# One large matmul for the prompt and one small one for the samples, in eight tiles of a feed-forward layer

## The chip, the cores and the metric

The kernel runs on one core of a Trainium2 chip, in one launch. The metric is the device time of that launch in microseconds (us). Before the change it is 1905.85 us, the median of three runs.

## The reference, cut to what matters

The model is a decoder step of two layers for a prompt of 512 tokens and 8 samples of one token each, with shared weights. Each layer has a mixer and, after it, a SwiGLU feed-forward; RMSNorm stands before and after every block. The change touches the feed-forward of layer 0 alone.

```python
D_MODEL = 1024; SEQ = 512; DEC_BATCH = 8; DEPTH = 2
D_FF = -(-8 * D_MODEL // (3 * 256)) * 256          # 2816

def swiglu(h, w_gate, w_up, w_down):
    return (jax.nn.silu(h @ w_gate) * (h @ w_up)) @ w_down

# in the trunk, for every layer l
x = x + rmsnorm(m, norm_mix_post[l])
f = swiglu(rmsnorm(x, norm_ffn_pre[l]), w_ffn_gate[l], w_ffn_up[l], w_ffn_down[l])
x = x + rmsnorm(f, norm_ffn_post[l])
```

## The kernel before, in words

**Layout.** Activations lie feature-major: 128 features on the partitions, tokens along the free axis. The tokens are 520 columns, 512 of the prompt and 8 of the samples, worked on in two halves: columns 0 to 255 (256 wide) and columns 256 to 519 (264 wide, so the samples ride with the second half). `HALF` and `HW` (lines 24 and 25) hold these.

**Precision.** Every linear layer is done in three products to keep nearly full precision: weights and inputs are each split into hi + lo, both of type float32r (fp32r; the profile's matmul rows write f32), and hi'xh + hi'xl + lo'xh is summed. The inputs of the feed-forward lie in the buffers Hh (hi) and Hl (lo).

**A linear layer, `lin` (line 299).** One output tile is 128 output features for all tokens. Over the 8 row tiles of the 1024 inputs, over the three products, and over the two halves, one matmul each: 8 x 3 x 2 = 48 a tile, into two PSUM accumulators, one for each half. The weights are the stationary operand (128x128) and the tokens the moving one; each matmul instruction comes with its own weight load, and both halves of a product use the same weights, one right after the other. The accumulators come from `acc` (line 261): a ring of four PSUM buffers of 512 float32 a partition, a tile takes two of them. All matmuls are recorded at line 268, that of the helper `mm`.

**Weights, `WStream` (line 129).** SP loads weights in blocks of 1 MB, 256 output columns (two tiles) at a time, into a ring of two buffers (raw, line 138). ACT or DVE rounds 4 row tiles of them to hi (whi, lines 289 and 290), POOL or DVE makes lo (wlo, line 165); both rings have four buffers. To every few loads a copy of the samples' key and value caches, DRAM to DRAM, is tied on SP's queue (`copy_after`, line 1122).

**The feed-forward, `ffn` (line 1059).** It has 22 gate tiles and 22 up tiles, in 11 steps p of two tiles t each: gate tiles 2p and 2p + 1, then up tiles 2p and 2p + 1. The four tiles of p = 0 are made ahead by `group` (line 308), the first halves of all before the second halves. Gate tile t = 2 goes to a spare PSUM buffer, ma (`spare`, line 1076, with `ma_f0`); all later ones go to acc. After a gate tile, for each half: DVE multiplies it by the tokens' norm (line 1095), ACT takes silu of it (line 1097). After an up tile, for each half: DVE multiplies it by the gate's (line 1104), ACT rounds that to hi (line 1106), DVE makes lo (line 1107). In the profile these stand under the helpers' lines, 274 (`tt`) and 284 (`act`). The output projection `out_proj` (line 469) follows, with w_ffn_down.

**What sets the order.** The program is written in one order; a planner of the tile framework (`schedule_with_timeline_sim=True`, line 1882) sets the order on each engine by dependencies and modelled times. `high_priority` pulls the weight splits and the reads of PSUM ahead, `issue_after` holds an instruction behind another. TensorE's matmuls of this stage stand in the written order.

Of the kernel before, what the change touches and what calls it, by code (L numbers as in the profile page):

```python
# [11 lines left out]
F32R = mybir.dt.float32r  # L12
# [109 lines left out]
def KN(n, v, *others):  # L122
    """The engine, share or order chosen at a place: v unless the table has another of the choices."""
    return KNOBS.get(n, v)
# [4 lines left out]
class WStream:  # L129
    """Weights, in the order of use: loaded in groups, split into hi + lo in units of at most 4 row tiles."""  # L130
# [38 lines left out]
    def tile(s, ap, c0, kts, spread=None, ncol=None, out=None):  # L169
        """Yield (row tile, hi, lo) for the 128 columns from c0 and the row tiles kts; input weights come two tiles a load.  # L170
        out = (buffer, offset) of 1024 floats for each four row tiles, to hold them apart from the ring."""
        if ncol is None:
            g = c0 - c0 % 256
            if s.key != (ap.tensor.name, ap.offset, g):
                s.key, s.raw = (ap.tensor.name, ap.offset, g), s.load(ap, 0, 8, g, 256)
            raw, off = s.raw, c0 - g
        else:
            raw, off = s.load(ap, 0, 8, c0, ncol), 0
        for k0 in range(0, len(kts), 4):
            hi, lo = s.split(raw, kts[k0], 4, off, spread, out and out[k0 // 4])  # L180
            for j in range(4):
                yield kts[k0] + j, hi[:, j], lo[:, j]

    def rows(s, ap, c0, loads):
        """As tile() for a tall matrix; loads are (first row tile, count, unit offsets in their order)."""
        for k0, n, offs in loads:
            raw = s.load(ap, k0, n, c0, 128)
            for o in offs:
                m = min(4, n - o)
                hi, lo = s.split(raw, o, m, 0)  # L190
                for j in range(m):
                    yield k0 + o + j, hi[:, j], lo[:, j]


class Ker:
# [14 lines left out]
    def gen(s, *names):  # L210
        """From here on these buffers hold something else: float32r operands and float32 data never share a tile."""
        for n in names:
            s.big[n] = s.sb.tile([128, BIG[n]], F32, tag=n, name=n, bufs=1)

    def lay(s, name, off=0, n=KD, dt=F32R):
        """Operand (tile, half) -> columns, for n tiles of all tokens."""
        t = s.B(name, off, n, NT, dt=dt)
        return lambda k, h: t[:, k, HALF[h]]

    def layh(s, name, n=KD):  # L220
        """As lay(), the first half of the tokens of every tile before the second."""
        return lambda k, h: s.B(name, 256 * n * h + k * HW[h], HW[h], dt=F32R)
# [63 lines left out]
    def cp(s, e, out, in_):  # L286
        """Copy on ACT, DVE or GpSimd."""
        if e == "A":
            return s.nc.scalar.copy(out, in_).ins  # L289
        return (s.nc.vector if e == "V" else s.nc.gpsimd).tensor_copy(out, in_).ins  # L290
# [7 lines left out]
    # ---- linear layers: weights stationary, 520 token columns moving in two halves  # L298
    def lin(s, w, xh, xl, nkt, halves=(0, 1), ps=None):
        """ps[half] = sum over row tiles of w (yielding (row tile, hi, lo)) of hi'xh + hi'xl + lo'xh."""  # L300
        ps = ps or {h: s.acc()[:, 0:HW[h]] for h in halves}
        for n, (kt, hi, lo) in enumerate(w):
            for lhs, x, st, sp in ((hi, xh, n == 0, False), (hi, xl, False, False), (lo, xh, False, n == nkt - 1)):
                for h in halves:
                    s.mm(ps[h], lhs, x(kt, h), st, sp)
        return ps

    def group(s, w, xh, xl, nkt):
        """Up to four tiles, the first half of the tokens of all before the second half, which may come later."""
        w = [list(v) for v in w]  # L310
        ps = [{} for _ in w]
        for t in range(len(w)):
            if t % 2 == 0:
                a = s.acc()
            ps[t][0] = a[:, 256 * (t % 2):256 * (t % 2) + 256]
        for t in range(len(w)):
            ps[t][1] = (s.acc() if t < 2 else s.mx())[:, 0:HW[1]]
        for h in (0, 1):
            for t, v in enumerate(w):
                s.lin(v, xh, xl, nkt, (h,), ps[t])  # L320
        return ps

    def lnexp(s, ins):
        """After ins, one table load for Ln and Exp."""
# [3 lines left out]
    def rstd(s, out, ps, n, e=EPS, keep=None, after=None):  # L328
        """out = rsqrt(ps / n + e), refined by a Newton step; keep = EPS * (ps / n + e)."""
# [17 lines left out]
    # ---- setup  # L347
# [66 lines left out]
    def add_sq(s, h, x, first, tmp, eng=None):  # L414
        """accT += x^2."""
# [7 lines left out]
    def prenorm(s, n, l, hi, lo, h, upd=None):  # L423
        """hi + lo = x * gain, exactly split."""
# [9 lines left out]
    def token_norm(s, h, keep=None):  # L434
        """s.R2 = per-token rsqrt(mean x^2 + eps), on every partition."""
# [7 lines left out]
    def boundary(s, deferred):  # L443
        """x += mp * rsqrt(mean m^2 + eps), then the next layer's prenorm (n, l, hi, lo): the second half, and the norms."""
# [5 lines left out]
    def residual(s, deferred, h):  # L450
        """One half's update of x, as a function of the feature tile."""
# [17 lines left out]
    def out_proj(s, rows, xh, xl, nkt, mp, n, l, pre, tail=2, final=False):  # L469
        """mp = m * gain, accT + sqs = sum m^2 for the eight tiles of an output projection; the last ones by token halves."""  # L470
# [46 lines left out]
    # ---- causal convolution of one 128-feature tile, then silu  # L517
# [26 lines left out]
    def conv_sample(s, nt, new, old, w, bias, out, tmp):  # L544
        """new [128, nt, 8], old [128, nt, 8, 3], w(j) [128, nt]; out [128, nt, 8] = silu(conv)."""
# [12 lines left out]
    def gate_z(s, ps, zt):  # L558
        """zt = silu(z)."""
# [8 lines left out]
    def softplus(s, out, x, n):  # L568
        """out = max(x, 0) + log1p(exp(-|x|)); log1p(e) = 2 atanh(e / (2 + e)) as a series. Shapes [128, n]."""
# [16 lines left out]
    # ---- layer 0: input projection and mixers in the order of issue  # L586
# [78 lines left out]
    # ---- layer 0: sample convolution state  # L665
# [21 lines left out]
    # ---- layer 0: dt, decays in token layout  # L687
# [53 lines left out]
    # ---- layer 0: SSD over four chunks of 128 tokens, for one group of heads  # L741
# [78 lines left out]
    # ---- layer 0: one SSM step per sample  # L820
# [39 lines left out]
    # ---- layer 0: gate, grouped norm  # L860
# [6 lines left out]
    def l0_norm(s, g, zt, yh, yl):  # L867
        """y * silu(z) (in zt), normalised, to the exactly split yh + yl."""
# [11 lines left out]
    # ---- layer 0: attention of the prompt  # L880
# [25 lines left out]
    def l0_tokens(s, hp):  # L906
        """Keys and values token-major: the caches of the prompt and of the samples, V for the products."""
# [82 lines left out]
    # ---- layer 0: attention of the samples over their cached rows  # L990
# [67 lines left out]
    # ---- SwiGLU  # L1058
    def ffn(s, l):
# [4 lines left out]
        x = s.lay("Hh"), s.lay("Hl")  # L1064

# [21 lines left out]
        for p in range(11):  # L1087
            sg = {}
            for t in (2 * p, 2 * p + 1):
                ps = first[t] if p == 0 else s.lin(s.W.tile(g, 128 * t, kts), *x, 8, ps=spare(t < 2 + KN("ma_f%d" % l, 0, 1, 2)))  # L1090
                for h in (0, 1):
                    sl = (s.B("cs", NT * (t % 2), NT) if l == 0 else sgs if t % 2 else s.accT)[:, HALF[h]]
                    gt = s.tmp(HW[h])
                    with s.tc.high_priority():
                        s.tt(gt, ps[h], s.R2[:, HALF[h]], ALU.mult)
# [3 lines left out]
            for t in (2 * p, 2 * p + 1):  # L1099
                ps = first[2 + t] if 2 + t < len(first) else s.lin(s.W.tile(u, 128 * t, kts), *x, 8)  # L1100
                for h in (0, 1):
                    gt = s.tmp(HW[h])
                    with s.tc.high_priority():
                        s.tt(gt, sg[t, h], ps[h], ALU.mult)
# [9 lines left out]
    def cache_shift(s):  # L1114
        """The samples' rolling caches: all rows but the oldest move up by one."""
# [11 lines left out]
    def final_early(s):  # L1127
        """x and the norm's eps of the second half token-major."""
# [27 lines left out]
    def final_first(s):  # L1156
        """The first half's outputs; m of the second half token-major, as far as it is known."""
# [26 lines left out]
    def final_last(s):  # L1184
        """The second half's outputs, token-major: x + m * rsqrt(mean m^2 + eps)."""
# [19 lines left out]
    # ---- layer 1: gated delta net, input projection and mixer in the order of issue  # L1205
# [119 lines left out]
    def vo(s, g, h, j):  # L1325
        """Half h of the tokens of v head 8 g + j: V token-major, then the outputs feature-major."""
# [5 lines left out]
    # ---- layer 1: beta, decays in token layout  # L1332
# [41 lines left out]
    # ---- layer 1: keys (w = 0) and queries token-major: sums of squares, keys for the state products  # L1374
# [23 lines left out]
    def log_norm(s, g, w):  # L1398
        """-log(sum of squares + eps) / 2 in place, seen per v head."""
# [6 lines left out]
    def bcast_rows(s, t, tag):  # L1406
        """[tokens, 32] to DRAM as 32 rows of 128 tokens."""
# [14 lines left out]
    # ---- layer 1: the 32 (chunk, v head) systems of one half of the heads, I + strictly lower  # L1422
# [37 lines left out]
    # ---- layer 1: transposed unit-triangular inverses in place of the systems: diagonal blocks of 32 by elimination  # L1460
# [27 lines left out]
    # ---- layer 1: the inverses of 64 and 128 rows from those of 32  # L1488
# [57 lines left out]
    # ---- layer 1: delta rule over four chunks of 128 tokens, for one half of the heads  # L1546
# [119 lines left out]
    # ---- layer 1: silu(z) times the normalised outputs, split into hi + lo  # L1666
# [16 lines left out]
    # ---- layer 1: sample convolution state  # L1683
# [25 lines left out]
    # ---- layer 1: one delta-rule step per sample: what the states are not needed for  # L1709
# [42 lines left out]
    # ---- layer 1: one delta-rule step per sample: outputs, then (l1_sample_state) states  # L1752
# [133 lines left out]
```

## Time and profile before

| what | value |
|---|---|
| median of 3 runs | 1905.85 us (1904.42 to 1915.31) |
| profiled execution, span from the first to the last instruction | 1901.6 us |
| the same execution's time from end to end | not given by the page |
| mean granted TensorE clock | 0.965 |
| DMA, mean rate | 141 GB/s |
| HBM, read and written | 241.01 MB and 62.04 MB |

How to read the profile: PE is TensorE's matmul, PEld its weight load, DVE VectorE, ACT ScalarE, POOL GpSimd, SP SyncE. A row of instructions gives line, engine, operation, the tiles written and read (out<-in), their shapes (`128*128 128x256`: loaded weights of 128 rows and 128 columns, 256 columns moving), and their count (x). In the timeline the first number is the start and the second the length of the merged piece, both in us; instructions of one name that follow one another are merged into one row with the shape of the first, so that a pair of 256 and 264 columns shows as 256 x2. In the groups by form the numbers behind the bar are busy us, mean ns of one, and idle us before them. A matmul's recorded length holds its way through the array, and matmuls overlap: how fast they follow one another is read from starts and counts, not from that length. A recorded end is modelled.

### The profile page before, as it was taken

The page shows a single profiled execution, that of the slowest core. Times are in us where ns is not written, and L with a number is a line of the kernel's source. Part 1 is how long each engine was busy: PE and PEld are TensorE (multiplying, and loading weights), DVE is VectorE, ACT ScalarE, POOL GpSimd, SP SyncE. Part 2 cuts the span into 40 slices and gives each one's busy share as a digit, 9 for nine tenths or more (in the row PEclk, how much of TensorE's full clock was granted, in tenths as well). Part 3 has the DMA queues.
Part 4 walks back from the last instruction along what each step waited for, and adds up shares of the span by engine and source line. Part 5 has one row for each costly group of instructions (what it writes and reads, how often), then busy time and mean ns, then how long its engine had stood idle before and what let it go on. Part 6 is the DMA issues. An engine that isn't in the chain of part 4 may idle for free.

```text
span 1901.6 us, 36269 instructions
## 1 busy us (share of the span) xinstructions
PE 1746.8 (92%) x14263; PEld 1659.2 (87%) x14263; DVE 1190.0 (63%) x2334; ACT 748.7 (39%) x1828; POOL 876.2 (46%) x768
## 2 busy tenths in 40 slices
PE   8899999898999999988968898989889999999996
PEld 7888777698999999977857787978889899999996
DVE  6898878638323221178899977888954954443125
ACT  5432335555222223355756555544334511111222
POOL 2565756234444433435474554646668411112452
PEclk9999999998999999999988899999989899999998
DMA  7345765453333334453442123257998333432333
GB/s 259 125 130 183 237 202 142 145 182 113 111 111 112 112 106 136 124 177 114 137 139 72 59 65 92 63 156 212 272 290 237 132 135 134 134 133 84 92 92 106
DMA packets 293323, 268.88 MB, mean 141 GB/s; under 512 B 11841, under 2 KB 276742, under 8 KB 291986
## 3 DMA queue, kind: packets, MB, share of 16 engines
q1 hardware_dynamic: 292502, 265.90, 45.5%
q8 instruction: 112, 1.84, 0.4%
q10 hardware_dynamic: 652, 0.68, 0.1%
q14 instruction: 57, 0.47, 0.1%
HBM read 241.01 MB, written 62.04 MB: 159 GB/s over the span
## 4 chain that ended last, share of the span: by engine, by line
PE 56%; DVE 26%; DMA 8%; issue 4%; ACT 4%; POOL 2%; SPq 1%; DVEq 0%; POOLq 0%; ACTq 0%
PE acc L268 48%; DVE p L274 4%; DVE cs L281 4%; PE ma L268 4%; PE mb L268 3%; DVE b L274 2%; DVE sq L281 2%; DMA raw<-in_w_ffn_down_dram 2%; DVE p L281 1%; DVE Hh L281 1%; PE mb L271 1%; DVE cs L274 1%; DMA bm<-csd 1%; POOL cs L274 1%; DVE wlo L165 1%
## 5 line engine op out<-in xcount | busy, mean ns | idle before, releaser
L165 POOL TENSOR_TENSOR wlo<-raw,whi 128x512 fp32r<-128x512 f32 (+3 forms) x373 | 500.8, 1346 | 676.7 <-ACT whi L289 368.1
L268 PE MATMUL acc<-Hl,whi 128*128 128x256 f32 (+1 forms) x2576 | 565.6, 291 | 20.2 <-DVE Hl L281 8.5
L268 PEld LDWEIGHTS acc<-Hl,whi 128*128 128x128 f32 x2576 | 420.5, 193 | 35.4 <-issue 11.3
L289 ACT CAST whi<-raw 128x512 fp32r<-128x512 f32 (+3 forms) x392 | 234.4, 602 | 453.0 <-PE acc L268 388.2
L268 PE MATMUL acc<-Hh,whi 128*128 128x256 f32 (+1 forms) x1824 | 387.0, 287 | 3.5 <-DVE cs L274 2.0
L268 PE MATMUL acc<-Hh,wlo 128*128 128x256 f32 (+1 forms) x1824 | 389.0, 288 | 0.0
L268 PEld LDWEIGHTS acc<-Hh,whi 128*128 128x128 f32 x1824 | 292.5, 191 | 8.2 <-issue 5.1
L268 PEld LDWEIGHTS acc<-Hh,wlo 128*128 128x128 f32 x1824 | 292.8, 191 | 7.5 <-issue 6.7
L268 PE MATMUL acc<-bm,whi 128*128 128x256 f32 (+1 forms) x1136 | 237.1, 290 | 1.4 <-DVE bm L281 1.4
L268 PE MATMUL acc<-p,whi 128*128 128x264 f32 (+1 forms) x1280 | 230.6, 287 | 4.4 <-ACT p L1819 1.6
L290 DVE CAST whi<-raw 128x512 fp32r<-128x512 f32 x131 | 61.1, 467 | 256.7 <-PE acc L268 195.2
L165 DVE TENSOR_TENSOR wlo<-raw,whi 128x512 fp32r<-128x512 f32 (+1 forms) x150 | 117.5, 785 | 142.2 <-ACT whi L289 138.8
L268 PEld LDWEIGHTS acc<-p,whi 128*128 128x128 f32 x1280 | 190.6, 192 | 6.4 <-ACT p L1819 1.9
L268 PEld LDWEIGHTS acc<-bm,whi 128*128 128x128 f32 x1136 | 182.1, 193 | 3.7 <-issue 1.6
L268 PE MATMUL acc<-p,wlo 128*128 128x256 f32 (+1 forms) x704 | 164.4, 288 | 8.7 <-DVE wlo L165 7.0
L268 PE MATMUL acc<-Hl,wlo 128*128 128x256 f32 (+1 forms) x752 | 171.1, 293 | 1.0 <-POOL wlo L165 0.9
L268 PEld LDWEIGHTS acc<-Hl,wlo 128*128 128x128 f32 x752 | 126.4, 195 | 3.2 <-POOL wlo L165 1.6
L268 PEld LDWEIGHTS acc<-p,wlo 128*128 128x128 f32 x704 | 119.6, 192 | 10.1 <-DVE wlo L165 7.9
L281 DVE SCALAR_TENSOR_TENSOR cs<-cs,cw 128x512 f32<-128x512 f32 x100 | 96.4, 966 | 12.7 <-POOL cs L274 8.6
L268 PE MATMUL acc<-X,whi 128*128 128x264 f32 (+1 forms) x512 | 100.4, 291 | 1.7 <-DVE X L274 1.3
L268 PEld LDWEIGHTS acc<-X,whi 128*128 128x128 f32 x512 | 80.4, 195 | 3.2 <-DVE X L274 1.6
L281 DVE SCALAR_TENSOR_TENSOR Hh<-cs,CS,Hh 128x256 f32<-128x256 f32 x64 | 53.1, 894 | 26.5 <-POOL Hh L274 26.2
(465 smaller groups left out, 2932.6 us busy)
## 6 DMA issues: line engine op xcount, KB each, us to landing
raw<-in_w_gdn_in_dram SPq DMA_DIRECT2D x24, 1024.0 KB
raw<-in_w_ffn_gate_dram SPq DMA_DIRECT2D x22, 1024.0 KB
raw<-in_w_ffn_up_dram SPq DMA_DIRECT2D x22, 1024.0 KB
raw<-in_w_ffn_down_dram SPq DMA_DIRECT2D x20, 1024.0 KB
raw<-in_w_hyb_in_dram SPq DMA_DIRECT2D x16, 1024.0 KB
out_sv_dram<-in_cache_attn_v_dram SPq DMA_DIRECT2D x16, 1023.0 KB
out_sk_dram<-in_cache_attn_k_dram SPq DMA_DIRECT2D x16, 1023.0 KB
raw<-in_w_gdn_out_dram SPq DMA_DIRECT2D x10, 1024.0 KB
```

What stands on the lines that cost most here:

```text
L165: eng.tensor_tensor(out=lo[:, :nk, d:d + n], in0=raw[:, :, o:o + n], in1=hi[:, :nk, d:d + n].bitcast(F32), op=ALU.subtract)
L268: s.nc.tensor.matmul(out, lhsT=lhsT, rhs=rhs, start=start, stop=stop, skip_group_check=skip)
L271: s.nc.tensor.transpose(out, in_, s.ident[0:in_.shape[0], 0:in_.shape[0]])
L274: return (eng or s.nc.vector).tensor_tensor(out=out, in0=a, in1=b, op=op).ins
L281: return s.nc.vector.scalar_tensor_tensor(out=out, in0=a, scalar=sc, in1=b, op0=op0, op1=op1).ins
L289: return s.nc.scalar.copy(out, in_).ins
L290: return (s.nc.vector if e == "V" else s.nc.gpsimd).tensor_copy(out, in_).ins
```

## The change

For p = 4 and 5 in layer 0, that is gate and up tiles 8 to 11, eight tiles in all, a new function `lin_wide` takes the place of `lin`. It makes the same three products over the same 8 row tiles, but its two matmuls a product take columns 0 to 511 and 512 to 519. The accumulators are one whole PSUM buffer for the prompt and 8 columns of another for the samples. The code that reads them still works by halves: the first half is read from the first 256 columns of the large accumulator, the second in two pieces, 256 columns from the large one and 8 from the small one. `lin_wide` takes the inputs as whole buffers (`xw`). The other lines of the diff blank out docstrings and comments.

```diff
+    def lin_wide(s, w, xh, xl, nkt):
+
+        a, b = s.acc(), s.acc()[:, 0:NS]
+        for n, (kt, hi, lo) in enumerate(w):
+            for lhs, x, st, sp in ((hi, xh, n == 0, False), (hi, xl, False, False), (lo, xh, False, n == nkt - 1)):
+                s.mm(a, lhs, x[:, kt, 0:NP], st, sp)
+                s.mm(b, lhs, x[:, kt, NP:NT], st, sp)
+        return {0: [(0, a[:, 0:256])], 1: [(0, a[:, 256:512]), (256, b)]}
...
         x = s.lay("Hh"), s.lay("Hl")
+        xw = [s.B(n, 0, KD, NT, dt=F32R) for n in ("Hh", "Hl")]
...
             for t in (2 * p, 2 * p + 1):
-                ps = first[t] if p == 0 else s.lin(s.W.tile(g, 128 * t, kts), *x, 8, ps=spare(t < 2 + KN("ma_f%d" % l, 0, 1, 2)))
+                wide = l == 0 and p in (4, 5)
+                if wide:
+                    ps = s.lin_wide(s.W.tile(g, 128 * t, kts), *xw, 8)
+                else:
+                    ps = first[t] if p == 0 else s.lin(s.W.tile(g, 128 * t, kts), *x, 8, ps=spare(t < 2 + KN("ma_f%d" % l, 0, 1, 2)))
                 for h in (0, 1):
...
                     with s.tc.high_priority():
-                        s.tt(gt, ps[h], s.R2[:, HALF[h]], ALU.mult)
+                        for c, v in ps[h] if wide else [(0, ps[h])]:
+                            c1 = c + v.shape[1]
+                            s.tt(gt[:, c:c1], v, s.R2[:, HALF[h]][:, c:c1], ALU.mult)
...
             for t in (2 * p, 2 * p + 1):
-                ps = first[2 + t] if 2 + t < len(first) else s.lin(s.W.tile(u, 128 * t, kts), *x, 8)
+                if wide:
+                    ps = s.lin_wide(s.W.tile(u, 128 * t, kts), *xw, 8)
+                else:
+                    ps = first[2 + t] if 2 + t < len(first) else s.lin(s.W.tile(u, 128 * t, kts), *x, 8)
                 for h in (0, 1):
...
                     with s.tc.high_priority():
-                        s.tt(gt, sg[t, h], ps[h], ALU.mult)
+                        for c, v in ps[h] if wide else [(0, ps[h])]:
+                            c1 = c + v.shape[1]
+                            s.tt(gt[:, c:c1], sg[t, h][:, c:c1], v, ALU.mult)
```

## The prediction

> **What bounds the kernel now.** I read the page first, for the engine that sets the end, then the stretches of the changed stage, then what TensorE waits for there, and last single weight loads.
>
> ```profile
> span 1901.6 us, 36269 instructions
> PE 1746.8 (92%) x14263; PEld 1659.2 (87%) x14263; DVE 1190.0 (63%) x2334; ACT 748.7 (39%) x1828; POOL 876.2 (46%) x768
> ...
> PE 56%; DVE 26%; DMA 8%; issue 4%; ACT 4%; POOL 2%; SPq 1%; DVEq 0%; POOLq 0%; ACTq 0%
> ```
>
> There are as many weight loads (PEld) as matmuls (PE), 14263 of each: a second matmul on the same weights loads them again. TensorE holds most of the chain. The chain of waits between 440 and 700 us, and what TensorE waited for between 430 and 700 us, show the feed-forward of layer 0:
>
> ```profile
> 467.44 5.78 PE ma L268 x48
> 473.22 226.81 PE acc L268 x1888
> ```
> ```profile
> PE acc L268 <- DVE Hl L281: 5.5, 4, 2.3
> ```
>
> The gate tile t = 2 is the one that goes to the buffer ma, 48 matmuls in 5.78 us. From 473.22 us on the chain is one unbroken run of matmuls: 1888 in 226.81 us, 120.1 ns each. The only waits (5.5 us) belong to the entry of the stage, where DVE still writes Hl. A tile takes 48 x 120.1 ns = 5.77 us. After t = 2, the other gate tile, two up tiles and the two whole steps p = 2 and 3 make 11 tiles, so p = 4 and 5, the changed ones, lie about 536.7 to 582.8 us:
>
> ```profile
> core 0: us, PE busy (x) PEld busy (x) DVE busy (x) ACT busy (x) POOL busy (x), PEclk, DMA share, GB/s
> 536.70:582.80 46.10, 46.10 (x386) 46.10 (x385) 14.02 (x31) 12.04 (x27) 20.63 (x16) 1.00 0.36 115
> ```
>
> TensorE is busy all 46.10 us at a granted clock of 1.00; DVE works 30% of it, ACT 26%, POOL 45%, the DMA engines 36%. Nothing waits beside TensorE, so a nanosecond added to its stream is a nanosecond added to the end, and a nanosecond saved is saved until the next engine binds.
>
> **The change part by part.** For each of 8 tiles, 8 row tiles and 3 products (192 in all), a pair of 256 and 264 columns becomes a pair of 512 and 8. The count of matmuls and loads stays: 384 each. Columns stay too: 520 a pair. What moves is how much streaming each load has to hide behind.
>
> *Removed: the old pair.* 2 x 120.1 = 240.2 ns. How it splits into streaming and a fixed part comes from a plain f32 matmul of 512 columns and the forms of the stage (third number: mean ns of one):
>
> ```profile
> 117.61 1.12 PE L268 MATMUL mb<-X 128*128 128x512 f32 x2 [0.54 <-DVE X L274]
> ```
> ```profile
> 117.61 0.30 PEld L268 LDWEIGHTS mb<-X 128*128 128x128 f32 x2 [0.75 <-DVE X L274]
> 118.14 0.19 PEld L268 LDWEIGHTS acc<-Hh,wlo 128*128 128x128 f32 x1 [0.24 <-issue]
> 118.57 0.31 PEld L268 LDWEIGHTS acc<-Hh,whi 128*128 128x128 f32 x2 [0.24 <-issue]
> ```
> ```profile
> L268 PE MATMUL acc<-Hh,wlo 128*128 128x264 f32 x98 | 27.8, 284 | 0.0
> L268 PE MATMUL acc<-Hh,wlo 128*128 128x256 f32 x98 | 27.6, 281 | 0.0
> ```
>
> The second of two plain f32 512-column matmuls streams from 118.14 to 118.57 us, 0.43 us or 0.83 ns a column. In the stage's fp32r form 8 more columns cost 3 ns, 0.4 ns each, and 260 columns take 120.1 ns in all, far under 0.83 each: so it streams at half the plain cost, 0.417 ns a column. 260 columns are 108.4 ns; 11.7 ns of a matmul's 120.1 are fixed.
>
> *Added: the wide matmul.* No row has fp32r at 512 columns. From below: streaming alone, 213.5 ns, nothing fixed. From above: the whole 120.1 ns in proportion, 236.5 ns. I take one fixed part, 213.5 + 11.7 = 225.2 ns, since 256 and 264 columns differ by streaming alone and the load that goes on behind a matmul is the same one. This term alone saves 15 ns a pair.
>
> *Added: the narrow matmul.* Eight columns stream 3 ns, so it costs what the next load costs, which has nothing left to hide behind. Full loads beside short matmuls stand in three places, and loads of few columns (128*8) in one; first the matmuls, then their loads:
>
> ```profile
> 905.74 0.66 PE L268 MATMUL mb<-small,cst 128*128 128x64 f32 x4 [0.54 <-DVE small L281]
> ...
> 1892.77 0.36 PE L268 MATMUL mb<-cst,acc 128*128 128x1 f32 x2
> ...
> 1893.29 0.20 PE L268 MATMUL mb<-cst,acc 128*8 128x1 f32 x2
> ...
> L268 PE MATMUL acc<-CS,cst 128*128 128x64 f32 x2 | 0.3, 248 | 0.0
> ```
> ```profile
> 905.74 0.52 PEld L268 LDWEIGHTS mb<-small,cst 128*128 128x128 f32 x4 [0.75 <-DVE small L281]
> ```
> ```profile
> 1892.53 0.30 PEld L268 LDWEIGHTS mb<-cst,sd 128*128 128x128 f32 x2
> 1892.74 0.30 PEld L268 LDWEIGHTS mb<-cst,acc 128*128 128x128 f32 x2
> 1892.97 0.30 PEld L268 LDWEIGHTS mb<-cst,sd 128*128 128x128 f32 x2
> 1893.29 0.10 PEld L268 LDWEIGHTS mb<-cst,acc 128*8 128x8 f32 x2
> 1893.32 0.11 PEld L268 LDWEIGHTS mb<-cst,sd 128*8 128x8 f32 x2
> ```
> ```profile
> 1201.48 0.30 PEld L268 LDWEIGHTS acc<-CS,cst 128*128 128x128 f32 x2
> 1201.70 0.30 PEld L268 LDWEIGHTS acc<-Hl,whi 128*128 128x128 f32 x2
> ```
>
> At 1892.7 us matmuls of one column (128x1, load of 128 columns) follow each other by 0.23 us a pair, 115 ns each; at 905.7 us four with 64 columns take (0.52 - 0.19) / 3 = 110 ns each. With 8-column weights the same one-column matmul goes about every 25 ns. So a full load that hides behind nothing costs some 111 ns, whatever little is streamed. The load at 1201.70 us is one of the weight stream (whi), behind a 64-column matmul, and the next starts 0.30 - 0.19 = 0.11 us later: fp32r weights load no faster. From below 25 ns (the floor without a load), from above 120.1 ns (a pair's half now). I take 111.5 ns, by the rows of the same full load.
>
> Why does the load not start earlier, behind the 225 ns of the wide one? At 118.14 us one load starts with the 0.43 us matmul and the next only at 118.57, when that has ended, though it idled 0.24 us. One load runs ahead, not two: the wide matmul hides the narrow one's load, and the next wide one's must wait until the narrow one has begun.
>
> *Sum.* 225.2 + 111.5 - 240.2 = +96.5 ns a pair; x 192 = +18.5 us. The stage's 46.1 us become 64.6. The bounds: 213.5 + 25 - 240.2 = -1.7 ns, -0.3 us; 236.5 + 120.1 - 240.2 = +116.4 ns, +22.3 us.
>
> The Trainium skill (TensorE: Matmul & The Clock Gate, Part 3, The mechanism) says that a load overlaps a running matmul only when it goes to other rows of the array. By it the old pair would be 2 x 111.5 + 217 = 440 ns and the new one the same, so no change. The trace disagrees, 120.1 ns a matmul being less than load and stream end to end over a run of 1888, so this rule gets no chance below. The same page (Back-to-back issue gap) gives some 131 ns as the sustained spacing at 512 columns; by it the new pair would be 131 + 111.5 = 242.5 ns, +0.4 us in all. The trace has only the plain 512-column matmul, at 0.43 us, and no fp32r one.
>
> *Moved: the results' way out.* Each tile's second half is read out in two DVE instructions, 256 and 8 columns, in place of one of 264: 8 more instructions.
>
> ```profile
> L274 DVE TENSOR_TENSOR sq<-acc,R 128x256 f32<-128x256 f32 x4 | 1.7, 422 | 8.4 <-PE acc L268 8.4
> L274 DVE TENSOR_TENSOR sq<-acc,R 128x264 f32<-128x264 f32 x4 | 1.7, 422 | 0.0
> ```
>
> An extra one costs between nothing and 422 ns, at most 3.4 us of DVE in 46 us of which it idles 32; I take nothing on the path. The bank of 512 columns is freed after two such reads, 0.84 us, in place of one. A tile still takes two of four acc buffers, so the tile that needs that bank starts a whole tile (5.8 us, then 8.1) later: covered. Were that gone, 0.42 us a tile, 3.4 us.
>
> *Moved: loads, splits, copies.* The weight loads of SP, the hi/lo splits on ACT, DVE and POOL and the cache copies tied to loads keep their order and come later, since their buffers free later. They idle in this stage and only gain slack. Planning may set other engines' instructions in another order; I take 0, with 1 to 2 us either way.
>
> **Against which time.** The sum is made on the span of 1901.6 us; the median of the runs, 1905.85, is 4.25 us above it, start and end around the span, which the change doesn't touch. 1905.85 + 18.5 = 1924.4 us.
>
> **The rivals.**
> 1. *Two loads run ahead* (not slower). Two loads (2 x 111.5 = 223 ns) would just fit behind the wide 225 ns; then the narrow one adds its 3 ns and the fixed 11.7, the pair is 240 ns: 1905.9 us. For it: TensorE is never idle and all loads are queued early. It decides from the point where a second load can start before the narrow matmul does. Against it: the load at 118.57 us.
> 2. *Wide streams go faster than by column* (the skill's 131 ns): +0.4 us, 1906.3. Against it: the 0.4 ns for each of 8 more columns.
> 3. *The bare load is half as long* (58 ns, as the load of half as many columns would be): 225.2 + 58 - 240.2 = 43 ns, +8.3 us, 1914.1. Against it: the row at 1201.70 us.
> 4. *The clock drops*, since the array streams only 217 of 337 ns. At the stage's entry, after an idle TensorE, the granted clock was 0.50 and 11 matmuls took 2 us where 18 do at 1.00:
>
> ```profile
> 444.00:446.00 2.00, 2.00 (x11) 2.00 (x11) 1.97 (x4) 0.06 (x1) 0.81 (x1) 0.50 0.06 7
> ...
> 458.00:460.00 2.00, 2.00 (x18) 2.00 (x18) 2.00 (x6) 1.18 (x3) 1.03 (x1) 1.00 0.00 0
> ```
>
> With the pair at 18/11 of 337 ns, 551 ns, it is +60 us: 1966. Against it: 904 to 907 us, where TensorE is busy 2.46 of 3.00 us, with the four bare loads of above, and keeps its 1.00:
>
> ```profile
> 904.00:907.00 3.00, 2.46 (x21) 2.25 (x21) 3.00 (x9) 1.61 (x5) 0.10 (x1) 1.00 0.17 48
> ```
>
> 5. *It isn't done as written*: the 512 columns come out as two matmuls of 256, each with a load: 2 x (106.7 + 11.7) + 111.5 - 240.2 = 108 ns, +20.8 us, 1926.6. Against it: the 512-column matmuls at 117.6 us are one instruction each.
>
> **How the numbers follow.** The forecast has 0.82, with its own range of 1919 to 1930: the wide one between 213.5 and 236.5 ns with the bare load (+16.3 to +20.7 us), an upper load of 120.1 ns (+22.3), and the planning and run noise of 2 us. Rival 1 has 0.06, 2 0.02, 3 0.04, 4 0.03, 5 0.01; 0.02 stays for a luckier order elsewhere. 1%, about what a measurement of this kernel can tell from no change, is 19.06 us, 1924.9: the forecast lies just under it. A fixed part that is smaller for a wide matmul (it was next to nothing in the plain one) pulls down, a second fixed part on the narrow one pulls up; I give 0.45 of the 0.82 to within 1% and 0.37 to slower. With rivals 1 to 3 within 1% is 0.57; with 4 and 5 slower is 0.41; faster 0.02. The range is 1914 to 1931: it takes in rival 3 and leaves out 1, 2, 4 and the tails.
>
> **What would show it.** In the profile after: 384 fp32r matmuls of new shapes, 128x512 and 128x8, 192 each; the eight tiles' stretch some 64.6 us long with TensorE's loads showing gaps behind each wide matmul's first 0.19 us; two loads 111 ns apart around each narrow matmul, then 225 ns to the next; the clock still 1.00; DVE with 8 more instructions and more idle time; everything after it the same, 18.5 us later. It is wrong if two loads start within one wide matmul, if the 8-column step is near 25 or 58 ns, if the wide one takes near 213 or 237, or if the stretch grows by 18 us and the span doesn't.

## The result, and the profile after

The changed kernel is slower. It took 1936.54 us (median of four runs) against 1907.82 us for the kernel before, run beside it: a ratio of 1.0141, 95% interval 1.0114 to 1.0169. A second session gave 1.0134 (1.0120 to 1.0147) on a median of 1910.61 us before, which is 25.6 us (22.9 to 28.1). The forecast was +18.5 us with a range that ended at +25.

The profiled execution of the changed kernel took 1933.21 us; its span is 1931.3 us, so 1.9 us lie around it. From the page of the changed kernel, span, busy time of each engine and the engines' shares of the chain that ended last:

```profile
span 1931.3 us, 36262 instructions
PE 1770.6 (92%) x14263; PEld 1674.0 (87%) x14263; DVE 1186.5 (61%) x2342; ACT 749.8 (39%) x1828; POOL 873.2 (45%) x768
...
PE 54%; DVE 20%; DMA 5%; ACT 3%; issue 3%; POOL 1%; SPq 0%; DVEq 0%; POOLq 0%; ACTq 0%
```

The span grew by 29.7 us, TensorE's busy time by 23.8 only, with the same 14263 matmuls: some of the time is not in the changed matmuls. DVE has the 8 more instructions. The chain of waits of the changed kernel in layer 0's feed-forward, then the stretch of the eight tiles:

```profile
464.84 5.78 PE ma L268 x48
470.61 289.45 PE acc L268 x2245
```
```profile
core 0: us, PE busy (x) PEld busy (x) DVE busy (x) ACT busy (x) POOL busy (x), PEclk, DMA share, GB/s
533.90:599.70 65.80, 65.80 (x387) 57.50 (x386) 14.09 (x37) 12.79 (x27) 20.56 (x16) 1.00 0.25 81
```

It is still one unbroken run of matmuls, at a granted clock of 1.00. The stretch of the eight tiles is 65.80 us in place of 46.10. From start to start, that is from the first wide matmul (533.87 us) to the first matmul behind the eight tiles (599.61 us), it is 65.74 us; the same tiles took 46.13 before (536.48 to 582.61 us), so they cost 19.6 us more. TensorE's loads (PEld) are busy 57.50 of the 65.80 us: in each pair there is a gap behind the second load, the narrow matmul's, while the wide matmul streams. The loads one by one (start, length of two that follow one another):

```profile
550.23 0.30 PEld L268 LDWEIGHTS acc<-Hh,whi 128*128 128x128 f32 x2
550.57 0.30 PEld L268 LDWEIGHTS acc<-Hl,whi 128*128 128x128 f32 x2
550.91 0.30 PEld L268 LDWEIGHTS acc<-Hh,wlo 128*128 128x128 f32 x2
551.25 0.30 PEld L268 LDWEIGHTS acc<-Hh,whi 128*128 128x128 f32 x2
551.60 0.19 PEld L268 LDWEIGHTS acc<-Hl,whi 128*128 128x128 f32 x1
```

Four pairs take 551.60 - 550.23 = 1.37 us, 342.5 ns a pair. One load is recorded at 0.19 us, so within a row of two the second starts 0.30 - 0.19 = 0.11 us after the first; from there to the next row it is 0.23 us. I read the 0.11 us as the wide matmul waiting for its own load, which starts only with the narrow matmul, and the 0.23 us as the wide matmul's stream; the run of wide matmuls alone, below, bears out the 0.23. 192 x (342.5 - 240.2) = 19.6 us, the growth of the stretch. The two new shapes, of one product (540 to 595 us; the third number is the mean ns of one):

```profile
L268 PE MATMUL acc<-Hh,whi 128*128 128x512 f32 x54 | 25.9, 480 | 0.0
L268 PE MATMUL acc<-Hh,whi 128*128 128x8 f32 x54 | 9.1, 168 | 0.0
```

The other 10 us of the span lie outside the tiles, and layer 1's mixer accounts for them. SP's weight loads mark it: from the first load of w_gdn_in to the last of w_gdn_out (rows: shortest, median and longest issue in ns, then first and last start in us). First before, then after:

```profile
L296 SPq DMA_DIRECT2D raw<-in_w_gdn_in_dram x25: 367/373/1319, 830.3 to 1336.8; - x25
L296 SPq DMA_DIRECT2D raw<-in_w_gdn_out_dram x10: 372/715/1132, 1348.2 to 1462.8; - x10
```
```profile
L296 SPq DMA_DIRECT2D raw<-in_w_gdn_in_dram x25: 367/373/1947, 847.1 to 1368.6; - x25
L296 SPq DMA_DIRECT2D raw<-in_w_gdn_out_dram x10: 372/626/1132, 1380.8 to 1492.1; - x10
```

632.5 us before (830.3 to 1462.8), 645.0 after (847.1 to 1492.1), 12.5 more. The span's 29.7 us are these 12.5, 16.8 ahead of the mixer (830.3 to 847.1: the tiles' 19.6, less the 2.6 by which this execution was earlier at gate tile 2, 467.44 against 464.84, and 0.2 of rounding and scatter) and 0.4 behind it. No line of that mixer was edited. But the two built programs, compared engine by engine, differ there: TensorE's instructions stand in the same order up to the eight tiles and behind them until the 7332nd of 13238 matmuls, in the middle of layer 1's mixer (it runs at 1070.5 us before); from there on some 75 blocks of them stand elsewhere. On DVE, ACT, POOL and SP, too, instructions of that mixer stand elsewhere. The planner orders by modelled times; that the new matmuls change these times for it is the likely reason, not a tested one.

### The profile page after: what moved, and what is told of

Its sections match the earlier page's. It is cut to its first block, busy times and chain, and to the rows that moved or that the text cites. A ratio compares the mean times of both kernels' runs of the same rounds, so it can differ in the third digit from the quotient of the medians.

```text
span 1931.3 us, 36262 instructions
## 1 busy us (share of the span) xinstructions
PE 1770.6 (92%) x14263; PEld 1674.0 (87%) x14263; DVE 1186.5 (61%) x2342; ACT 749.8 (39%) x1828; POOL 873.2 (45%) x768
## 4 chain that ended last, share of the span: by engine, by line
PE 54%; DVE 20%; DMA 5%; ACT 3%; issue 3%; POOL 1%; SPq 0%; DVEq 0%; POOLq 0%; ACTq 0%
PE acc L268 48%; PE ma L268 4%; DVE p L274 3%; DVE cs L281 2%; PE mb L268 2%; DVE b L274 2%; DMA raw<-in_w_ffn_down_dram 2%; DVE sq L281 1%; DVE Hh L281 1%; DVE p L281 1%; DVE p L1478 1%; DVE Hh L274 1%; PE mb L271 1%; DVE cs L274 1%; ACT L284 1%
## 5 line engine op out<-in xcount | busy, mean ns | idle before, releaser
L268 PE MATMUL acc<-Hl,whi 128*128 128x256 f32 (+3 forms) x2576 | 570.9, 293 | 21.3 <-DVE Hl L281 9.2
L268 PE MATMUL acc<-Hh,whi 128*128 128x256 f32 (+3 forms) x1824 | 391.6, 290 | 3.5 <-DVE cs L274 2.0
L268 PE MATMUL acc<-Hh,wlo 128*128 128x256 f32 (+3 forms) x1824 | 393.3, 290 | 0.0
L281 DVE SCALAR_TENSOR_TENSOR cs<-cs,cw 128x512 f32<-128x512 f32 x100 | 95.8, 960 | 11.7 <-POOL cs L274 7.6
L281 DVE SCALAR_TENSOR_TENSOR Hh<-cs,CS,Hh 128x256 f32<-128x256 f32 x64 | 48.8, 821 | 34.6 <-POOL Hh L274 20.1
```

The lines of the kernel that those rows point to most:

```text
L268: s.nc.tensor.matmul(out, lhsT=lhsT, rhs=rhs, start=start, stop=stop, skip_group_check=skip)
L281: return s.nc.vector.scalar_tensor_tensor(out=out, in0=a, scalar=sc, in1=b, op0=op0, op1=op1).ins
```

## The experiments

There are two theories. The *order theory*: the eight tiles cost 19.6 us by themselves, and the rest is the new order of layer 1's mixer. The *stage theory*: all of it comes from the tiles and what runs late behind them, and the new order is harmless. A ratio is turned into us on the median of before in its own session, 1908.96 us for the first four kernels and 1910.61 us for the last four.

**One tile alone.** Layer 1's order comes out exactly as in the changed kernel, with an eighth of the wide matmuls.

```diff
-                wide = l == 0 and p in (4, 5)
+                wide = l == 0 and t == 8          # gate tile; the up tiles: False
```

> Only gate tile 8 of layer 0 has the wide and the narrow matmul. The order in which layer 1's work is issued is the same as in the changed kernel, and another than before the change. Order theory: the tile costs 24 x 102 ns = 2.4 us more, and the new order of layer 1 costs its whole 12 to 13 us: 14 to 16 us above before (about 0.8%), with the down projection's loads of layer 0 2.4 us later and those of layer 1 some 15 us later. Stage theory (everything comes from the eight tiles and from what runs late behind them): an eighth of 27 us, 3 to 4 us.

Measured: 1.0060 (1.0046 to 1.0075), 11.5 us (8.8 to 14.3). An eighth of 19.6 is 2.5, so 9.0 us (6.3 to 11.8) are left for the order. The stage theory's 3 to 4 us lie far outside; the order theory's 14 to 16 was also too high at the median, as its 12 to 13 us came from one pair of profiles, and the mixer's time varies from run to run. The mixer's marks in this profile, 642.6 us apart:

```profile
L296 SPq DMA_DIRECT2D raw<-in_w_gdn_in_dram x25: 367/375/1420, 836.2 to 1356.3; - x25
L296 SPq DMA_DIRECT2D raw<-in_w_gdn_out_dram x10: 372/648/1142, 1367.4 to 1478.8; - x10
```

**The same eight tiles in layer 1's feed-forward.** Everything else is issued in the order of before.

```diff
-                wide = l == 0 and p in (4, 5)
+                wide = l == 1 and p in (4, 5)
```

> The same eight tiles, but in the feed-forward of layer 1; all other work is issued in the order of before. Both theories agree on the tiles: 192 pairs, each 102 ns longer. Order theory: 19.6 us more (18 to 21), all of it within the eight tiles, and nothing after them: 1.0%. Stage theory: 27 us more as in layer 0, since what runs behind a late stage pays again.

Measured: 1.0111 (1.0097 to 1.0125), 21.2 us (18.5 to 23.9). The order theory's 19.6 is inside, 27 is outside. The stretch of the tiles is the same as in layer 0, to the digit (65.74 us from start to start here too); then the mixer's marks:

```profile
1586.70:1652.50 65.80, 65.80 (x387) 57.50 (x385) 24.01 (x59) 6.58 (x16) 6.45 (x5) 1.00 0.28 96
```
```profile
L296 SPq DMA_DIRECT2D raw<-in_w_gdn_in_dram x25: 367/373/1407, 828.5 to 1340.9; - x25
L296 SPq DMA_DIRECT2D raw<-in_w_gdn_out_dram x10: 372/518/1133, 1352.0 to 1467.2; - x10
```

The mixer took 638.7 us here, 6.2 more than in the profile of before, with the same order. That is how far single profiles scatter, and why "nothing outside the tiles" can't be read from this one. The mixer also stands ahead of these tiles, so this run doesn't tell what it would lose by running late; the two kernels with an idle matmul, below, do.

**The wide matmul alone.** The narrow matmuls of the eight tiles are left out, and the reads of the samples' columns take columns of the large accumulator.

```diff
-        a, b = s.acc(), s.acc()[:, 0:NS]
+        a = s.acc()
...
-                s.mm(b, lhs, x[:, kt, NP:NT], st, sp)
-        return {0: [(0, a[:, 0:256])], 1: [(0, a[:, 256:512]), (256, b)]}
+        return {0: [(0, a[:, 0:256])], 1: [(0, a[:, 248:512])]}
```

> Leaves out the narrow matmuls of the eight tiles, so the samples' columns are not computed there; 512-column matmuls follow one another, each load behind a full stream. Theory of a fixed part: 225 ns each (213.5 + 11.7). Theory in proportion to the columns: 233 to 237 ns each, as they took in the changed kernel. A third theory, that the narrow one disturbs the wide: near 216 here. The eight tiles last 192 x that: 43.2, 44.7 to 45.5 or 41.5 us.

Measured: the loads follow each other with the matmuls,

```profile
559.86 0.19 PEld L268 LDWEIGHTS acc<-Hh,whi 128*128 128x128 f32 x1
...
561.50 0.19 PEld L268 LDWEIGHTS acc<-Hl,whi 128*128 128x128 f32 x1
```
```profile
539.90:584.50 44.60, 44.60 (x194) 36.02 (x193) 13.88 (x30) 12.19 (x26) 20.70 (x16) 1.00 0.36 119
```

The two rows are the first and the last of eight: 1.64 us / 7 = 234 ns; over the whole stretch, 44.60 us / 192 = 232 ns. It lies at the lower edge of the proportional theory; neither a fixed part of 11.7 ns over 213.5 (225 ns) nor a disturbance by the narrow matmul (216 ns) fits. (The kernel as a whole took 1925.28 us in its one run, with the new order of layer 1.)

**Another split.** The 520 columns are split into 384 and 136.

```diff
-        a, b = s.acc(), s.acc()[:, 0:NS]
+        a, b = s.acc(), s.acc()[:, 0:136]
...
-                s.mm(a, lhs, x[:, kt, 0:NP], st, sp)
-                s.mm(b, lhs, x[:, kt, NP:NT], st, sp)
+                s.mm(a[:, 0:384], lhs, x[:, kt, 0:384], st, sp)
+                s.mm(b, lhs, x[:, kt, 384:NT], st, sp)
-        return {0: [(0, a[:, 0:256])], 1: [(0, a[:, 256:512]), (256, b)]}
+        return {0: [(0, a[:, 0:256])], 1: [(0, a[:, 256:384]), (128, b)]}
```

> The eight tiles take 384 and 136 columns in place of 512 and 8. Load theory: the second matmul streams 57 ns, still less than a load, so it costs the bare load, 109 to 112 ns, just as 8 columns do; the first one 175 ns (between 118 at 256 and 233 at 512): the pair 284 to 288 ns, the eight tiles 54.5 to 55.3 us. Rival, a matmul of few columns streams at a quarter of the rate: 136 x 4 x 0.417 = 227 ns, the pair 402 ns, the eight tiles 77 us. Rival, only the number of columns counts: the pair 240 ns, 46.1 us.

Measured: the eight tiles last 54.90 us, 285.9 ns a pair, and the narrow one is again 0.30 - 0.19 = 0.11 us:

```profile
537.80:592.70 54.90, 54.90 (x386) 54.90 (x386) 14.34 (x37) 12.67 (x27) 20.61 (x16) 1.00 0.29 97
```
```profile
559.96 0.30 PEld L268 LDWEIGHTS acc<-Hh,whi 128*128 128x128 f32 x2
560.24 0.30 PEld L268 LDWEIGHTS acc<-Hl,whi 128*128 128x128 f32 x2
...
561.38 0.30 PEld L268 LDWEIGHTS acc<-Hh,wlo 128*128 128x128 f32 x2
```

136 columns cost as much as 8: the price is that of the load. Both rivals, 402 and 240 ns a pair, are out. (1928.03 us in its one run.)

**One and two matmuls more.** The kernel before gets, in gate tile 8, an idle matmul of 8 columns into a buffer that nobody reads; then two of them.

```diff
+                if l == 0 and t == 8:
+                    q = s.mx()
+                    for _ in range(1):            # the other kernel: 2
+                        s.mm(q[:, 0:8], s.ones, s.ident[:, 0:8])
```

> The kernel before, with one matmul of 8 columns more in gate tile 8 of layer 0, into a buffer that nobody reads: 0.1 us of TensorE. The planner then issues layer 1's work in another order than before, and another than the changed kernel's. Order theory: since the order of before is one of many and a good one, most others are slower, by an amount that isn't known beforehand: 3 to 15 us more, all of it in layer 1's mixer. Stage theory: 0.1 us, nothing that can be measured.

> The same with two such matmuls: 0.2 us of TensorE, and a third order of layer 1, nearer to that of before (21 places differ on TensorE, against 84 with one). Order theory: 0 to 10 us more, and another value than with one. Stage theory: 0.2 us, nothing that can be measured.

Measured: 1.0023 (1.0010 to 1.0035) with one, 4.4 us (1.9 to 6.7); 1.0031 (1.0019 to 1.0042) with two, 5.9 us (3.6 to 8.0). The added work is 0.1 and 0.2 us; the rest is what the new orders cost. Here nothing runs late by more than that and no tile is changed, so the stage theory has no place for it. The order that differs in fewer places costs no less. The mixer of the kernel with one, 641.8 us:

```profile
L296 SPq DMA_DIRECT2D raw<-in_w_gdn_in_dram x25: 367/373/1265, 830.9 to 1346.8; - x25
L296 SPq DMA_DIRECT2D raw<-in_w_gdn_out_dram x10: 372/874/1165, 1358.2 to 1472.7; - x10
```

**The split reads alone.** The matmuls have 256 and 264 columns as before, and the second half is read in two pieces.

```diff
-        a, b = s.acc(), s.acc()[:, 0:NS]
+        a, b = s.acc()[:, 0:256], s.acc()[:, 0:HN]
...
-                s.mm(a, lhs, x[:, kt, 0:NP], st, sp)
-                s.mm(b, lhs, x[:, kt, NP:NT], st, sp)
-        return {0: [(0, a[:, 0:256])], 1: [(0, a[:, 256:512]), (256, b)]}
+                s.mm(a, lhs, x[:, kt, 0:256], st, sp)
+                s.mm(b, lhs, x[:, kt, 256:NT], st, sp)
+        return {0: [(0, a)], 1: [(0, b[:, 0:256]), (256, b[:, 256:264])]}
```

> The matmuls are those of before, 256 and 264 columns, and only the eight tiles' second half is read out in two DVE instructions of 256 and 8 columns. All engines' order is that of before but for these 8 instructions. Both theories: the same time as before, within 1 us of mean, since DVE idles two thirds of the stage; the extra instructions last 100 to 420 ns each. A rival, the late release of the accumulators costs time: up to 3.4 us, seen as gaps in TensorE in the stage.

Measured: 1.0000 (0.9990 to 1.0010). The reads cost nothing that can be told from zero, and the rest of the program, whose order they leave alone, costs nothing more either. In the changed kernel such a read takes 154 ns (group by form, mean ns behind the comma):

```profile
L274 DVE TENSOR_TENSOR sq<-acc,R 128x8 f32<-128x8 f32 x4 | 0.6, 154 | 0.0
```

**The changed kernel again**, unedited, beside the last three.

> The changed kernel once more, beside the three others on one chip. Order theory: 19.7 us in the eight tiles and some 5 to 12 us in layer 1: 25 to 32 us, 1.3 to 1.7%, more than the 1.1% of the same tiles in layer 1. Stage theory: the same total, but without a share in layer 1's mixer that a lone reordering shows as well.

Measured: 1.0134 (1.0120 to 1.0147), 25.6 us (22.9 to 28.1). Less the tiles' 19.6, 6.0 us (3.3 to 8.5) are left for the order; with the one tile it was 9.0 (6.3 to 11.8). The two intervals overlap from 6.3 to 8.5. Over the profiles of all kernels the mixer, between the marks above, took 632.5, 635.3 and 638.7 us in the order of before; 642.6, 643.0, 645.0, 648.5 and 650.8 in that of the changed kernel; 641.8 and 642.1 in the two others. No profile with a new order is as short as the longest with the old one.

The same rows of SP's loads show where the time goes. From the mixer's first load to its twentieth (1154.3 us before, 1170.4 in the changed kernel), all ten profiles take 322.6 to 328.8 us, whatever the order and however late the mixer starts (324.0 before, 323.3 in the changed kernel, 16.8 us late). From the twentieth to the last load of w_gdn_in it is 182.5 to 186.4 us in the order of before, 197.0 to 200.7 in that of the changed kernel (197.0 with the one tile, which adds 2.4 us only), and 190.0 and 191.2 with the idle matmuls. What is left of the mixer takes 122 to 126 us in all ten. So the time is lost behind the first matmul that stands elsewhere, and it goes with the order and not with how late the mixer runs.

## Why the prediction was wrong, point by point

- *TensorE bounds the stage, and a nanosecond added to it is added to the end.* Right: there is one unbroken run of matmuls before and after, and the stretch grew by just what its pairs grew.
- *The narrow matmul costs a bare load, 111.5 ns, because one load runs ahead and not two.* Right in mechanism and nearly in size: it was 0.11 us for 8 columns and for 136, and 342.4 - 232.5 = 109.9 ns by the stretches with and without the narrow matmuls.
- *The wide matmul costs 213.5 + 11.7 = 225.2 ns.* Wrong in size: it took 232 to 234, near the upper bound of 236.5. The first step that failed is the division of 120.1 ns into a rate of 0.417 ns a column and a fixed part of 11.7. The rate was half of 0.83 ns a column, read off plain f32, and the halving rested only on 120.1 ns for 260 columns being far under that. Moreover, the two 512-column rows at 117.6 us are not two matmuls but the two records of one plain f32 instruction. (The built program of before has 13238 matmul instructions, 1025 of them plain f32; the profile counts 14263, one more for each of these.) A plain f32 matmul of 512 columns thus takes 2 x 0.43 = 0.86 us, and that half of one record came near the fp32r rate was luck. The 3 ns between 256 and 264 columns that propped it up are a difference over 8 columns only, between modelled lengths. Measured over more columns there is hardly a fixed part: 120.1 / 260 = 0.46, (285.9 - 110) / 384 = 0.46, 232 / 512 = 0.45 ns a column; a line through the first and the last is 0.44 ns a column and some 5 ns fixed, an estimate. Seven to nine ns in 192 pairs are 1.3 to 1.7 us; with a bare load slightly cheaper than taken, the tiles cost 19.6 us in place of 18.5.
- *Planning may set other engines' instructions in another order; I take 0, with 1 to 2 us either way.* Wrong, and the larger error; this is the step that took the result out of the range. The order of layer 1's mixer cost 6 to 9 us, and even a single idle matmul of 0.1 us brought an order that cost 4.4. I bounded the term by nothing that the profile shows, and called it noise of both signs. With the tiles' 19.6 us alone the result would have been 1925.5 on the forecast's base, within the range. Of the 12.1 us between the forecast of 1924.4 and the 1936.54 measured, 2.0 are the base (1907.82 in place of 1905.85), 1.1 the tiles, and some 9 are left for the order.
- *The split reads and the loads on their way out cost nothing.* Right: 1.0000 (0.9990 to 1.0010).
- *Rivals.* Two loads ahead, a half-price load, a dropped clock and a 512-column matmul that comes as two are all refuted by the pair of 342.5 ns, the clock of 1.00 and the 192 matmuls of each new shape. (The rows at 117.6 us, which the prediction held against the last of these, are of one plain f32 instruction with two records and say nothing on it.) The faster wide stream is refuted by 232 ns. The Trainium skill (TensorE: Matmul & The Clock Gate, Back-to-back issue gap) gives about 131 ns for 512 columns; the trace disagrees, with 232 ns. The same page of the Trainium skill (LDWEIGHTS (loading the stationary operand)) gives a load's time as the number of columns divided by 1.2, in ns, which makes 107 for 128 columns, an estimate; here the trace agrees, with 0.11 us.

It is left open why the new orders of the mixer are slower. The stretch in which the time is lost, between the same two of SP's loads, first before, then after:

```profile
1154.30:1336.80 182.50, 167.96 (x1330) 152.10 (x1331) 153.85 (x339) 93.87 (x280) 93.38 (x83) 0.98 0.49 140
```
```profile
1170.40:1368.60 198.20, 175.98 (x1343) 158.92 (x1344) 155.87 (x342) 95.57 (x283) 95.92 (x86) 0.94 0.44 129
```

It is 15.7 us longer, with about as many instructions; TensorE is busy 8.0 us longer and idle 7.7 us longer, at a lower granted clock (0.94 for 0.98). No single wait carries it. One lead is that in all five profiles with the changed kernel's order the chain of work in this stretch holds a wait of about 5 us for the load of the samples' convolution state (ex<-in_state_gdn_conv_dram, at 1171.34 us in the changed kernel), and in none of the three with the order of before; it was not tested, and with the idle matmuls, slower as well, that wait is 2.8 us with one and not on the chain with two. No mixer with one block of its order put back was run. Nor was the new tiles' effect on the whole time measured in layer 0 with the old order of layer 1: none of the variants built had both.

## What to carry to other kernels

In these runs every matmul carries its own weight load, and a matmul costs the larger of its stream and the next load: the load is 0.11 us, some 240 columns at 0.46 ns. Two halves of 256 and 264 columns hide both loads; 512 and 8 hide one and lay the other bare. And where a planner orders the whole program, an edit in one stage can draw a new order for stages behind it. It did for the changed kernel, the variants of it in layer 0 with other matmuls and both idle matmuls, and did not for the tiles in layer 1 and the split reads. Compare the built programs before believing that the rest only moves, and put that risk on the slow side when the order at hand is a good one: all three new orders seen here were slower.

## What the runs showed of the hardware that was not expected

At 256 to 512 columns and a granted clock of 1.00 the fp32r stream costs 0.45 to 0.46 ns a column, 232 ns for 512. A plain f32 matmul of 512 columns takes 0.86 us, in two records of 0.43 us with a load each, so fp32r costs a little over a quarter of it. A narrow fp32r matmul, 8 or 136 columns, showed no price of its own above the load's 0.11 us.
